# One pass of the index keys' projection folded into unused weight columns, and a turn of the heads' weights moved down the queue

## The chip, the cores and the metric

The kernel runs on one core of a Trainium2 chip. A core has five engines with an instruction queue each, run in order: TensorE (PE, with its weight loads PEld), VectorE (DVE), ScalarE (ACT), GpSimd (POOL) and SyncE (SP, which here only issues DMAs). Times are device microseconds (us) for one execution, from launch to end; lower is better. A profile shows one execution, and its span runs from the first to the last instruction.

## The reference

One transformer block on 512 tokens of width 1024, in float32. Its input projection `u @ w_in` is cut into the parts of three attentions; the second (DSA) is the one that matters here:

```python
aq, ak, av, bq, bkv, biq, bik, biw, cq, ck, cv, g = split_cols(u @ w_in[l])
...
s_idx = jax.nn.relu(jnp.einsum('bqhd,bkd->bqhk', iqb, ik))
score = jnp.einsum('bqhk,bqh->bqk', s_idx, iwb).astype(jnp.float32) * idx_scale
score = jnp.where(causal[None], score, -jnp.inf)
_, sel = lax.top_k(score, topk)
```

`biq` are the index queries (8 heads of 32 columns), `bik` the index keys (32 columns that all heads share), `biw` the weight of each head (8 columns). The scores choose which keys the DSA attention reads, so they are computed to nearly full float32. After the three attentions come their branch products, the output product, a feed-forward part and a last norm.

## The kernel before

Nearly all of the time goes to 128x512 matmuls in float32r. To keep precision, each projection is three passes: the weights and the activations are split into a high and a low half (`wh`, `wl`, `uh`, `ul`), and a pass is `wh*uh`, `wl*uh` or `wh*ul`, summed in one PSUM bank. ACT writes a high half by a copy into float32r, DVE the low half by subtraction.

**The first stage** takes the model dimension in four shares of two 128-row tiles. In a share q the modulation sums (`mod_sums`, DVE and ACT: eight scaled rows summed into `gsum`) are turned into columns by small matmuls (`gps`, L376), DVE makes the factors `ab` from them, ACT makes `uh`, splits the weights (`split_share`) and makes `ut`, DVE makes the low halves and `ul`, and PE runs `b_part` (L456) for three weight tiles of 256 columns: `b0` (banks `p_kv`, `p_iq0`), `b1` (banks `p_iq1`, `p_ik`) and `bq0` (banks `p_bq00`, `p_bq01`). Of the second 128 columns of `b1` only 40 are used: 32 index keys and 8 head weights; the other 88 are computed and read by nobody. While PE runs share q, DVE sums for share q+1.

**Behind the shares** stand, in program order: the copies of the index queries (`put_iq`, with 12 small DMAs each, half on SP and half on POOL, that lay heads side by side in `iqs`), the copies of `p_ik` (`kst` and `kl`, high and low half of the keys, with two DMAs that repeat them on partitions 32 to 95; `iwr`, the head weights), and the two banks of `bq0`. Then PE starts the chunk `bq1`: 48 matmuls (L535, L537, L539). Between them small steps are interleaved, by a queue that `Flow.run` empties:

```python
if self.side and i % 4 == 3:
    self.side.popleft()()
...
flow.side.extend([iw_turn, kv1, kv2, kv3, lambda: None, kv4, kv5])
```

So the first step stands behind the 4th matmul, the next behind the 8th, and so on. `iw_turn` turns the head weights `iwr` on PE (L596, bank tag T, which has one buffer) and copies them to `iw` on DVE. `kv1` turns `kvT` on PE (L612, bank T), `kv2` makes the squares and the root on ACT (L617, L619), `kv3` the reciprocal and `kvt` on DVE (L622, L624), `kv4` turns `kvt` back on PE (L630, bank T), `kv5` writes `kvnT` on DVE. The chunks `c0` to `c2` follow `bq1`, with the index products between their matmuls.

Of the kernel before, what the change touches and what calls it, by code (L numbers as in the profile page):

```python
# [13 lines left out]
F32 = mybir.dt.float32  # L14
F32R = mybir.dt.float32r
AF = mybir.ActivationFunctionType
ALU = mybir.AluOpType
# [109 lines left out]
def block_kernel(ctx: ExitStack, tc: tile.TileContext, x, c, rel_bias, ada_w, ada_b, norm_mix, w_in,  # L127
                 gate_b, diff_lambda, diff_subln, dsa_kv_norm, dsa_w_uv, w_br_a, w_br_b, w_br_c, w_o,
                 norm_mlp, w_ff1, w_ff2, norm_final, onehot, out):
    nc = tc.nc  # L130
# [12 lines left out]
    flow = Flow()  # L143
# [64 lines left out]
    raws, parts = {}, {}  # L208
# [80 lines left out]
    SHARES = ((0, 2), (2, 4), (4, 6), (6, 8))  # L289
# [108 lines left out]
    def split_share(q, names):  # L398
        ks = slice(*SHARES[q])
        for n in names:  # L400
            if n not in parts and n == "b1":
                both = st.tile([128, 2, 8, 256], F32R, name="hl_b1")
                parts[n] = (both[:, 0], both[:, 1])
            elif n not in parts:
                parts[n] = tuple(wp.tile([128, 8, 256], F32R, tag=t, name=f"{t}_{n}") for t in ("hi", "lo"))
            hi, lo = parts[n]
            nc.scalar.activation(hi[:, ks], raws[n][:, ks], AF.Copy)
            nc.vector.tensor_tensor(lo[:, ks], raws[n][:, ks], hi[:, ks].bitcast(F32), op=ALU.subtract)

# [36 lines left out]
    def b_part(n, q, ps=(0, 1, 2)):  # L446

        wh, wl = parts[QS[n]]
        names = (("kv", 0), ("iq0", 1)), (("iq1", 0), ("ik", 1)), (("bq00", 0), ("bq01", 1))
        for p in ps:  # L450
            w, u = ((wh, uh), (wl, uh), (wh, ul))[p]
            products = [(name, j, k) for name, j in names[n] for k in range(*SHARES[q])]
            if n == 0:
                products.sort(key=lambda e: e[2])
            for name, j, k in products:
                nc.tensor.matmul(first[name], w[:, k, j * 128:(j + 1) * 128], u[:, k],  # L456
                                 start=k == 0 and p == 0, stop=k == KT - 1 and p == 2)
                yield
# [10 lines left out]
    mod_columns(0)  # L469
    warm(5)  # L470
    split_share(0, QS[:1])
    make_uh(0)
    split_share(0, QS[1:])
    make_ul(0)
    mod_sums(1, range(4))

    def first_two(q):

        return chain(b_part(0, q, (0, 1)), b_part(1, q, (0, 1)), b_part(0, q, (2,)), b_part(1, q, (2,)))

    for q in range(LAST):
        if q + 2 <= LAST:
            fetch_share(q + 2)
        mod_sums(q + 1, range(4, KT))
        rest = b_part(2, q)
        for _ in chain(first_two(q), islice(rest, 4)):
            pass
        split_share(q + 1, QS[:1])
        if q + 2 <= LAST:
            mod_sums(q + 2, (0, 1))  # L490
        mod_columns(q + 1)
        make_uh(q + 1)
        if q + 2 <= LAST:
            mod_sums(q + 2, (2, 3))
        split_share(q + 1, QS[1:])
        make_ul(q + 1)
        if q + 1 == LAST:
            fetch(3)
            fetch(4)
        for _ in rest:  # L500
            pass
# [13 lines left out]
    def kv_tile(name, dt=F32):  # L515
        return at.tile([128, 512], dt, tag="kv", name=name, bufs=14)

    def p_tile(name, dt=F32):
        return at.tile([128, 512], dt, tag="P", name=name, bufs=5)
# [24 lines left out]
    def proj_chunk(chunk, evacs, when=(2, 5, 7, 12)):  # L544
        use(chunk, when)
        for j in range(2):
            yield from proj(f"p_{chunk}{j}", chunk, j, evacs[j])
# [4 lines left out]
    kst = at.tile([96, 512], F32R, tag="kst", name="kst")  # L552
    kl = p_tile("kl", F32R)
    iwr = p_tile("iwr")
    iw = const.tile([128, 32], F32, name="iw")

    def put_iq(g, p):
        nc.scalar.activation(iqx[:, 2 * g], p, AF.Copy)
        nc.vector.tensor_tensor(iqx[:, 2 * g + 1], p, iqx[:, 2 * g].bitcast(F32), op=ALU.subtract)
        for r in range(4):  # L560
            for b, part in enumerate((0, 1, 0)):
                (nc.gpsimd if r < 2 else nc.sync).dma_start(iqs[32 * b:32 * b + 32, 4 * g + r].bitcast(F32),
                                  iqx[32 * r:32 * r + 32, 2 * g + part, 128:512].bitcast(F32))
# [6 lines left out]
    kvT = kv_tile("kvT")  # L570
    nc.scalar.activation(kvT, first["kv"], AF.Copy)
    p_ik = first["ik"]
    nc.scalar.activation(kst[0:32], p_ik[0:32], AF.Copy)
    nc.vector.tensor_tensor(kl[0:32], p_ik[0:32], kst[0:32].bitcast(F32), op=ALU.subtract)
    nc.scalar.activation(iwr[32:40], p_ik[32:40], AF.Copy, scale=0.0625)
    nc.sync.dma_start(kst[32:64].bitcast(F32), kst[0:32].bitcast(F32))
    nc.sync.dma_start(kst[64:96].bitcast(F32), kl[0:32].bitcast(F32))
    put_iq(1, first["iq1"])
    for _ in b_part(2, LAST):
        pass  # L580

# [2 lines left out]
    def put_bq(i):  # L584
        def evac(p):
            bq[i] = kv_tile(f"bq{i}")
            nc.scalar.activation(bq[i], p, AF.Copy, scale=128 ** -0.5)
        return evac

    put_bq(0)(first["bq00"])  # L590
    put_bq(1)(first["bq01"])

    def iw_turn():
        iwp = bank("T", "iwp")
        for i in range(1, 4):
            nc.tensor.transpose(iwp[:, 8 * i:8 * i + 8], iwr[32:40, i * 128:(i + 1) * 128], ident[32:40, 32:40])  # L596
        nc.vector.tensor_copy(iw[:, 8:32], iwp[:, 8:32])
# [34 lines left out]
    def kv5():  # L632
        nc.vector.tensor_scalar(kvnT, kb["b"], vcol[:, C_KVN:C_KVN + 1], None, op0=ALU.mult)

    flow.side.extend([iw_turn, kv1, kv2, kv3, lambda: None, kv4, kv5])
    flow.run(proj_chunk("bq1", [put_bq(2), put_bq(3)], (14, 18, 26, 32)))


# [952 lines left out]
```

## Time and profile before

| | us |
|---|---|
| median of 3 runs (lowest to highest) | 834.23 (833.16 to 834.74) |
| the profiled execution's own time | 833.88 |
| its span | 832.0 |
| PE busy in the span | 806.9 (97%) |
| DVE, ACT, POOL busy | 570.3, 411.8, 163.6 |

The span is 1.88 us shorter than the execution's own time, which has what lies around the instructions. PE is the busiest engine by far: what delays PE's queue delays the end, unless PE would have waited anyhow. "Busy" counts a matmul from its start to its modelled end, so that back-to-back matmuls overlap; the distance from start to start is what a matmul costs PE.

### The profile page before, as it was taken

How to read it: one execution, taken by the hardware profiler on the slowest of the kernel's cores; microseconds unless marked ns; L12 is line 12 of the kernel's file. 1: busy time of each engine (PE TensorE's matmuls, PEld its weight loads, DVE VectorE, ACT ScalarE, POOL GpSimd, SP SyncE). 2: the span in 40 equal slices, each digit the busy share in tenths (PEclk: the TensorE clock that was granted, in tenths of full speed). 3: DMA queues.
4: the chain of work that ended last, by engine and by line, in shares of the span. 5: the costliest groups of instructions: out<-in, count | busy, mean ns of one | idle time of the engine just before them, and what ended most of it. 6: DMA issues, size and time to landing. Idle time of an engine off the chain costs nothing. (4 is left out here: it accounts for less than half of the span.)

```text
span 832.0 us, 10495 instructions
## 1 busy us (share of the span) xinstructions
PE 806.9 (97%) x3865; PEld 644.7 (77%) x3865; DVE 570.3 (69%) x1004; ACT 411.8 (49%) x712; POOL 163.6 (20%) x118
## 2 busy tenths in 40 slices
PE   5999999999999999999999999999999999999996
PEld 4778877678777776677788789888888888888885
DVE  5865776687878359894454776874678578857554
ACT  7555635452434365455743436545563366334433
POOL 2014332202562225003156460000000000010020
PEclk9999999999999999999999999999999999999998
DMA  9946552134656276421137527114411531173302
GB/s 313 347 134 189 190 196 74 52 102 127 198 183 213 96 267 191 153 89 52 50 103 265 187 68 290 50 51 154 151 50 51 189 129 37 52 252 102 101 1 101
DMA packets 81534, 116.47 MB, mean 140 GB/s; under 512 B 4590, under 2 KB 53274, under 8 KB 81484
## 3 DMA queue, kind: packets, MB, share of 16 engines
q1 hardware_dynamic: 78812, 107.73, 39.5%
q0 software_dynamic: 2672, 8.09, 2.8%
q8 instruction: 30, 0.49, 0.2%
q14 instruction: 20, 0.16, 0.1%
HBM read 110.25 MB, written 8.17 MB: 142 GB/s over the span
## 5 line engine op out<-in xcount | busy, mean ns | idle before, releaser
L1275 PE MATMUL pf<-u2h,hi_f 128*128 128x512 f32 x224 | 87.1, 389 | 0.0
L1277 PE MATMUL pf<-u2l,hi_f 128*128 128x512 f32 x224 | 87.1, 389 | 0.0
L1279 PE MATMUL pf<-u2h,lo_f 128*128 128x512 f32 x224 | 87.1, 389 | 0.0
L956 DVE SCALAR_TENSOR_TENSOR adacc<-adch,cond,adacc 128x512 f32<-128x512 f32 x56 | 59.7, 1065 | 5.2 <-DMA adch<-in_ada_w_dram 4.7
L244 DVE TENSOR_TENSOR lo_f<-raw_f,hi_f 128x1024 fp32r<-128x1024 f32 x38 | 46.6, 1255 | 16.9 <-ACT hi_f L232 16.9
L232 ACT ACTIVATE hi_p<-w 128x1024 fp32r<-128x1024 f32 x36 | 36.3, 1050 | 34.0 <-PE pp L1421 27.0
L244 DVE TENSOR_TENSOR lo_p<-w,hi_p 128x1024 fp32r<-128x1024 f32 x36 | 42.7, 1221 | 9.8 <-ACT hi_p L232 9.8
L232 ACT ACTIVATE hi_f<-raw_f 128x1024 fp32r<-128x1024 f32 x38 | 38.6, 1048 | 21.5 <-PE p2l L1537 7.1
L1279 PEld LDWEIGHTS pf<-u2h,lo_f 128*128 128x128 f32 x224 | 42.0, 188 | 8.8
L1277 PEld LDWEIGHTS pf<-u2l,hi_f 128*128 128x128 f32 x224 | 42.0, 188 | 8.7
L1275 PEld LDWEIGHTS pf<-u2h,hi_f 128*128 128x128 f32 x224 | 42.0, 188 | 8.7
L1445 POOL DMA_DIRECT2D x1f<-x1d x4 | 2.1, 538 | 234.3 <-PE pp L1421 234.3
L1421 PE MATMUL pp<-hi_p,hq 128*128 128x512 f32 x144 | 45.8, 389 | 0.0
L244 POOL TENSOR_TENSOR lo_gb<-raw_gb,hi_gb 128x1024 fp32r<-128x1024 f32 x8 | 20.0, 2524 | 66.0 <-ACT hi_gb L232 66.0
L1421 PEld LDWEIGHTS pp<-hi_p,hq 128*128 128x128 f32 x144 | 27.0, 188 | 5.6
L1421 PE MATMUL pp<-hi_p,ha 128*128 128x512 f32 x96 | 30.5, 389 | 0.0
L1421 PE MATMUL pp<-hi_p,he 128*128 128x512 f32 x96 | 30.5, 389 | 0.0
L735 ACT ACTIVATE Pa<-Pa,nma 128x128 f32<-128x128 f32 (+3 forms) x32 | 17.7, 554 | 24.6 <-DVE nma L731 24.5
L1415 DVE TENSOR_TENSOR acc<-acc,pp 128x512 f32<-128x512 f32 x32 | 21.7, 683 | 10.6 <-PE pp L1421 10.6
L1421 PE MATMUL pp<-lo_p,hq 128*128 128x512 f32 x72 | 28.1, 390 | 0.0
L535 PE MATMUL p_gb<-uh,hi_gb 128*128 128x512 f32 x64 | 27.5, 430 | 0.0
L537 PE MATMUL p_gb<-ul,hi_gb 128*128 128x512 f32 x64 | 26.8, 419 | 0.0
(430 smaller groups left out, 2300.1 us busy)
## 6 DMA issues: line engine op xcount, KB each, us to landing
raw_f<-in_w_ff_dram SPq DMA_DIRECT2D x20, 1024.0 KB, 5.7
adch<-in_ada_w_dram SPq DMA_DIRECT2D x64, 256.0 KB, 3.2
w<-in_w_ff_dram SPq DMA_DIRECT2D x12, 1024.0 KB
ada<-in_ada_w_dram SPq DMA_DIRECT2D x32, 256.0 KB, 6.4
raw_gc<-in_w_in_dram SPq DMA_DIRECT2D x4, 1024.0 KB, 16.9
raw_gb<-in_w_in_dram SPq DMA_DIRECT2D x4, 1024.0 KB, 5.6
raw_a<-in_w_in_dram SPq DMA_DIRECT2D x4, 1024.0 KB
raw_ga<-in_w_in_dram SPq DMA_DIRECT2D x4, 1024.0 KB, 7.6
```

The costliest lines, as they stand in the source:

```text
L232: nc.scalar.activation(parts[n][0][:, sl], raws[n][:, sl], AF.Copy)
L244: eng.tensor_tensor(parts[n][1][:, sl], raws[n][:, sl], parts[n][0][:, sl].bitcast(F32), op=ALU.subtract)
L535: nc.tensor.matmul(dst, wh[:, k, cs], uh[:, k], start=k == 0, stop=False)
L537: nc.tensor.matmul(dst, wh[:, k, cs], ul[:, k], start=False, stop=False)
L735: nc.scalar.activation(p[:, 0:w], p[:, 0:w], AF.Exp, bias=nm, scale=-1.0, accum_out=sm)
L956: nc.vector.scalar_tensor_tensor(acc, ach[n], cond[:, k:k + 1], acc, op0=ALU.mult, op1=ALU.add)
L1275: nc.tensor.matmul(dst, wh[:, i, cs], u2h[:, i], start=i == 0, stop=False)
L1277: nc.tensor.matmul(dst, wh[:, i, cs], u2l[:, i], start=False, stop=False)
L1279: nc.tensor.matmul(dst, wl[:, i, cs], u2h[:, i], start=False, stop=i == KT - 1)
L1415: nc.vector.tensor_tensor(c, c, dst[t], op=op)
L1421: nc.tensor.matmul(dst[t], a[:, part, k, j, ts_], w[:, k], start=not onto and k == 0 and m == 0, stop=k == 3 and m == 2, skip_group_check= ...
L1445: nc.gpsimd.dma_start(x1f[:, t], x1d[t * 128:(t + 1) * 128])
```

## The change

The split of tile `b1` now writes, into the 88 unused columns of the high tile, the low halves of the 40 used ones: columns 192 to 231 of the high tile hold the low half of columns 128 to 167, the rest of columns 168 to 255 is set to zero by POOL once. The first pass over `p_ik` then gives the high product on partitions 0 to 39 and the low product on partitions 64 to 103 of the same bank, and the pass `wl*uh` of `ik` is left out. The two parts have to be added: ACT copies partitions 64 to 103 to `ikl`, a DMA moves them to partitions 0 to 39, and DVE adds (`iks`). The copies that made `kst`, `kl` and `iwr` from `p_ik` now take `iks` (function `put_ik`) and stand behind the two copies of `bq0`. `iw_turn` goes from the front of the side queue to its end. (The third pass, `wh*ul`, now also has a low part; it is a product that was left out before.)

```diff
@@ split_share
+                nc.gpsimd.memset(both[:, 0, :, 168:256].bitcast(F32), 0.0)
...
+            if n == "b1":
+
+                for c0, c1, dst in ((0, 128, lo[:, ks, 0:128]), (128, 168, hi[:, ks, 192:232])):
+                    if c0 == 0:
+                        nc.scalar.activation(hi[:, ks, 0:168], raws[n][:, ks, 0:168], AF.Copy)
+                    nc.vector.tensor_tensor(dst, raws[n][:, ks, c0:c1], hi[:, ks, c0:c1].bitcast(F32), op=ALU.subtract)
+                continue
@@ b_part
-            products = [(name, j, k) for name, j in names[n] for k in range(*SHARES[q])]
+            products = [(name, j, k) for name, j in names[n] for k in range(*SHARES[q]) if (name, p) != ("ik", 1)]
@@ behind the shares
-    nc.scalar.activation(kst[0:32], p_ik[0:32], AF.Copy)
-    nc.vector.tensor_tensor(kl[0:32], p_ik[0:32], kst[0:32].bitcast(F32), op=ALU.subtract)
-    nc.scalar.activation(iwr[32:40], p_ik[32:40], AF.Copy, scale=0.0625)
-    nc.sync.dma_start(kst[32:64].bitcast(F32), kst[0:32].bitcast(F32))
-    nc.sync.dma_start(kst[64:96].bitcast(F32), kl[0:32].bitcast(F32))
+    ikl, iks = p_tile("ikl"), p_tile("iks")
+    nc.scalar.activation(ikl[64:104], p_ik[64:104], AF.Copy)
+    nc.sync.dma_start(ikl[0:40], ikl[64:104])
     put_iq(1, first["iq1"])
+
+    def put_ik():
+
+        nc.vector.tensor_tensor(iks[0:40], p_ik[0:40], ikl[0:40], op=ALU.add)
+        nc.scalar.activation(kst[0:32], iks[0:32], AF.Copy)
+        nc.vector.tensor_tensor(kl[0:32], iks[0:32], kst[0:32].bitcast(F32), op=ALU.subtract)
+        nc.scalar.activation(iwr[32:40], iks[32:40], AF.Copy, scale=0.0625)
+        nc.sync.dma_start(kst[32:64].bitcast(F32), kst[0:32].bitcast(F32))
+        nc.sync.dma_start(kst[64:96].bitcast(F32), kl[0:32].bitcast(F32))
+
...
     put_bq(1)(first["bq01"])
+    put_ik()
...
-    flow.side.extend([iw_turn, kv1, kv2, kv3, lambda: None, kv4, kv5])
+    flow.side.extend([kv1, kv2, kv3, lambda: None, kv4, kv5, iw_turn])
```

The change moves instructions on several queues. On SP, behind the last loads of the first stage, the queue was this (`iqs` are the small DMAs of the index queries, `kst` those of the keys):

```order
L217 DMA raw_c_510<-in_w_in_dram 128x8x256
L562 DMA iqs<-iqx 32x384 x6
L576 DMA kst<-kst 32x512
L577 DMA kst<-kl 32x512
L562 DMA iqs<-iqx 32x384 x6
L217 DMA raw_c_619<-in_w_in_dram 128x8x256
```

and is now this:

```order
L217 DMA raw_c_509<-in_w_in_dram 128x8x256
L570 DMA iqs<-iqx 32x384 x6
L583 DMA ikl<-ikl 40x512
L570 DMA iqs<-iqx 32x384 x6
L592 DMA kst<-kst 32x512
L593 DMA kst<-kl 32x512
L217 DMA raw_c_621<-in_w_in_dram 128x8x256
```

The new transfer of `ikl` stands behind the first six `iqs` transfers, where the first `kst` transfer stood, and the two of `kst` stand behind all twelve.

On ACT, from the copy of `p_kv` to the split of `c0`, before (`kjunk` are the squares of `kv2`):

```order
L571 ACTIVATE kvT<-p_kv 128x512
L573 ACTIVATE kst<-p_ik 32x512
L575 ACTIVATE iwr<-p_ik 8x512
L558 ACTIVATE iqx<-p_iq_245 128x512
L587 ACTIVATE bq_607<-p_bq_247 128x512
L587 ACTIVATE bq_609<-p_bq_248 128x512
L617 ACTIVATE kjunk,kss<-tpk 128x128 x4
L619 ACTIVATE kss<-kss,eps 128x4
```

and now:

```order
L579 ACTIVATE kvT<-p_kv 128x512
L582 ACTIVATE ikl<-p_ik 40x512
L566 ACTIVATE iqx<-p_iq_245 128x512
L603 ACTIVATE bq_603<-p_bq_247 128x512
L603 ACTIVATE bq_605<-p_bq_248 128x512
L589 ACTIVATE kst<-iks 32x512
L591 ACTIVATE iwr<-iks 8x512
L634 ACTIVATE kjunk,kss<-tpk 128x128 x4
L636 ACTIVATE kss<-kss,eps 128x4
```

The two copies out of the keys went from ahead of the second `iqx` copy to the place right ahead of the squares, and they read `iks`. On DVE the sum `iks` and the subtraction `kl` stand, in the same way, right ahead of the reciprocal of `kv3`.

On PE, from the first matmul of `bq1`, before:

```order
L535 MATMUL p_bq_621<-uh,hi_bq_568 128x512
L537 MATMUL p_bq_621<-ul,hi_bq_568 128x512
L539 MATMUL p_bq_621<-uh,lo_bq_569 128x512
L535 MATMUL p_bq_621<-uh,hi_bq_568 128x512
L596 MATMUL iwp<-ident,iwr 128x8 x3
L537 MATMUL p_bq_621<-ul,hi_bq_568 128x512
L539 MATMUL p_bq_621<-uh,lo_bq_569 128x512
L535 MATMUL p_bq_621<-uh,hi_bq_568 128x512
L537 MATMUL p_bq_621<-ul,hi_bq_568 128x512
L612 MATMUL tpk<-ident,kvT 128x128 x4
```

and now:

```order
L543 MATMUL p_bq_623<-uh,hi_bq_565 128x512
L545 MATMUL p_bq_623<-ul,hi_bq_565 128x512
L547 MATMUL p_bq_623<-uh,lo_bq_566 128x512
L543 MATMUL p_bq_623<-uh,hi_bq_565 128x512
L629 MATMUL tpk<-ident,kvT 128x128 x4
L545 MATMUL p_bq_623<-ul,hi_bq_565 128x512
L547 MATMUL p_bq_623<-uh,lo_bq_566 128x512
```

Every step of `kv` stands four matmuls of `bq1` earlier: the first turn behind 4 matmuls instead of 8, the turn back (`kv4`) behind 20 instead of 24, and the head weights' turn behind 28 instead of 4.

## Rows read from the trace of the kernel before

**Rows 1.** The page, part 1: busy us, share of the span, instructions.

```profile
PE 806.9 (97%) x3865; PEld 644.7 (77%) x3865; DVE 570.3 (69%) x1004; ACT 411.8 (49%) x712; POOL 163.6 (20%) x118
```

**Rows 2.** Waits of PE, whole span: us in total, times, longest.

```profile
PE u2p L1247 <- POOL tn L1242: 2.4, 2, 1.6
PE gps L376 <- DVE gsum L368: 2.3, 3, 1.8
```

**Rows 3.** Timeline of PE, first stage: start, us, instruction, idle before and releaser.

```profile
18.02 1.02 PE L376 MATMUL gps<-ones,gsum 128*128 128x1 f32 x8 [0.19 <-DVE gsum L368]
...
29.17 1.02 PE L376 MATMUL gps<-ones,gsum 128*128 128x1 f32 x8 [1.80 <-DVE gsum L368]
...
36.76 0.62 PE L456 MATMUL p_ik<-uh,hl_b 128*128 128x512 f32 x2
37.22 0.39 PE L456 MATMUL p_kv<-ul,hi_b 128*128 128x512 f32 x1
...
49.53 1.02 PE L376 MATMUL gps<-ones,gsum 128*128 128x1 f32 x8 [0.32 <-DVE gsum L368]
```

**Rows 4.** Groups by form, ACT and DVE: busy us, mean ns of one, idle before.

```profile
L407 ACT ACTIVATE hl_b<-raw_b 128x512 fp32r<-128x512 f32 x4 | 2.5, 614 | 0.0
L232 ACT ACTIVATE hi_bq<-raw_bq 128x1024 fp32r<-128x1024 f32 x2 | 2.0, 1050 | 0.0
L408 DVE TENSOR_TENSOR hl_b<-raw_b,hl_b 128x512 fp32r<-128x512 f32 x4 | 2.8, 693 | 5.2 <-ACT hl_b L407 5.2
L244 DVE TENSOR_TENSOR lo_bq<-raw_bq,hi_bq 128x1024 fp32r<-128x1024 f32 x2 | 2.4, 1223 | 0.3 <-ACT hi_bq L232 0.3
```

**Rows 5.** Timeline of PE, chunk bq1 up to the first matmul of c0.

```profile
60.51 0.39 PE L535 MATMUL p_bq<-uh,hi_bq 128*128 128x512 f32 x1
...
62.28 0.35 PE L596 MATMUL iwp<-ident,iwr 8*128 8x8 f32 x3 [0.71 <-ACT iwr L575]
...
67.87 0.60 PE L630 MATMUL tpk<-ident,kvt 128*128 128x128 f32 x4
...
68.55 0.39 PE L537 MATMUL p_bq<-ul,hi_bq 128*128 128x512 f32 x1
...
73.77 0.39 PE L535 MATMUL p_c<-uh,hi_c 128*128 128x512 f32 x1
```

**Rows 6.** Timeline of SP behind the shares: issue of the small DMAs.

```profile
57.71 3.78 SPq L562 DMA_DIRECT2D iqs<-iqx  x6
61.67 0.51 SPq L576 DMA_DIRECT2D kst<-kst  x1
```

**Rows 7.** Transfers of tile iqs (24 of 48 KB): issue to landing.

```profile
DMA to landing us min/median/max: 1.8/2.0/2.1
```

**Rows 8.** Timelines of ACT and of DVE behind the shares.

```profile
61.64 0.59 ACT L575 ACTIVATE iwr<-p_ik 8x512 f32<-8x512 f32 x1 [1.12 <-DVE kl L574]
...
64.42 0.28 ACT L617 ACTIVATE kjunk<-tpk 128x128 f32<-128x128 f32 x1 [0.58 <-PE tpk L612]
...
60.94 0.67 DVE L574 TENSOR_TENSOR kl<-p_ik,kst 32x512 fp32r<-32x512 f32 x1
...
66.56 1.13 DVE L624 TENSOR_SCALAR kvt<-tpk,kss 128x128 f32<-128x128 f32 x4
```

**Rows 9.** Windows of PE: stretch, length, busy (instructions), granted clock (1.00 is full), DMA share, GB/s.

```profile
27.00:31.00 4.00, 2.20 (x14) 1.00 1.09 348
31.00:35.00 4.00, 4.00 (x12) 0.57 1.09 347
479.00:483.00 4.00, 4.00 (x22) 1.00 0.02 4
824.30:826.60 2.30, 0.00 (x0) 1.00 0.55 204
826.80:832.00 5.20, 0.00 (x0) 0.50 0.53 199
```

**Rows 10.** A memset of POOL, in groups by form.

```profile
L600 POOL MEMSET cmask<- 128x512 f32 x1 | 0.5, 546 | 0.0
```

## Prediction

> **What bounds the kernel now.** I read the page first: PE is busy for 97% of the span [rows 1], so a change of 2 us has to be looked for in PE's queue. Next the waits of PE over the whole span: they are few, and two are long, the turn of `u2` far behind the change and the `gps` matmuls, which wait for DVE's sums in the first stage [rows 2]. The reader is to see there that the stage in which the matmuls are removed is one of the few in which PE waits. Then the timelines of PE: first the four shares, then the chunk `bq1`, in which PE stood 0.71 us for the head weights [rows 3, 5]; and those of SP, ACT and DVE behind the shares, to see what the new transfer waits for and who waits for it [rows 6, 8].
>
> **The matmuls removed.** Eight go, two in each share. The pair of the second share starts at 36.76 and the next matmul at 37.22 [rows 3]: 0.23 us each at full clock, 0.46 a share, 1.84 in all. How much of it arrives is another matter.
>
> Share 1. PE waits 1.80 us for `gsum` at 29.17 [rows 3]. Two matmuls less make that wait longer; what counts is when DVE is done. DVE's sums stand behind the low half of `b1`, for which DVE waits on ACT's copy in every share [rows 4]. That copy shrinks from 512 to 336 elements: from 614 ns at 512 and 1050 ns at 1024 [rows 4] an element costs 0.85 ns, so 0.15 us are saved. On DVE 512 elements become 256 and 80; from 693 and 1223 ns [rows 4], 1.04 ns an element, they cost 0.43 and 0.25, the same as the 0.69 before. So the wait ends 0.15 earlier: gain 0.15.
>
> Share 2. PE does not wait for `gsum` at its end: the three waits of [rows 2] are those at 18.02, 29.17 and 49.53 [rows 3]. The 0.46 arrives. Sum 0.6.
>
> Share 3. PE waited 0.32 us at 49.53 [rows 3], so DVE ended last, and again only ACT's 0.15 counts. Sum 0.75, and PE's wait there grows to about 0.6.
>
> Share 4. Nothing of DVE stands between: 0.46 arrives. Sum 1.2. So `bq1`, which began at 60.51 [rows 5], begins at 59.3. Bounds: 0.9 (second share DVE-bound too) and 1.84 (no wait at all).
>
> POOL's memset (704 elements; 546 ns for 512 [rows 10], so some 0.75 us by proportion) lies in POOL's idle time before the first use of the tile. I take it at nothing; if DVE's sums stood still for all of it, the first share would begin 0.75 later.
>
> **The turn moved.** At `iw_turn` PE stood 0.71 us and worked 0.35 [rows 5]. Behind the 28th matmul the weights are there, and only the 0.35 is paid. That saves 0.7, if nothing else waits.
>
> **What is added.** `iks` needs both parts on the same partitions, so the path is ACT copy, SP issue, transfer, DVE sum. The transfer takes the slot in SP's queue in which `kst` was issued, at 61.67, because the six `iqs` issues ahead of it take 3.78 us [rows 6]. They wait for `iqx`, which moves with PE: 61.67 - 1.2 = 60.47. ACT's copy of `ikl` is ready before that. Of its landing no row shows anything; the nearest is that of `iqs`, 1.8 to 2.1 us from the issue for 48 KB [rows 7]. It carries 80 KB, so I take the upper end, 2.1: 62.57. [...]
>
> Then DVE adds: 0.67 like `kl`, which reads the same bank [rows 8], to 63.24. ACT now has the copies `kst` and `iwr` right ahead of the squares of `kv2`, and its queue is in order: two operations of the length of `iwr` (0.59 each [rows 8], less some 0.09 by which neighbours overlap) end the wait of the squares at 63.28 + 1.0 = 64.28. Before they began at 64.42, and `kvt` ended at 66.56 + 1.13 = 67.69 [rows 8], 3.27 later. So now `kvt` ends at 67.55, and the turn back (`kv4`), which stood 0.18 behind it, starts at 67.7. That is hardly earlier than the 67.87 of before [rows 5].
>
> But PE comes to it much earlier, since it now stands behind 20 matmuls, not 24, and no longer behind the head weights. A group of four transposes costs 68.55 - 67.87 - 0.23 = 0.45 [rows 5]. PE arrives at 59.3 + 20 x 0.227 + 0.45 = 64.3 and stands till 67.7: by the trace's way of counting (to a matmul's modelled end, 0.16 more) **an idle time of about 3.2 us**. Queued behind the waiting transposes are the 28 other matmuls of `bq1` and everything after. ACT's squares wait for `kst`, `kst` for `iks`, `iks` for the transfer: that is the new chain.
>
> From there to the first matmul of `c0`: 0.45 + 28 x 0.227 + 0.35 = 7.16, so 74.86, against 73.77 [rows 5]. **The removed work and the removed wait are paid back with 1.1 us on top.** Break-even needs the turn back at 66.6, 1.1 us earlier than I have it.
>
> Later needs have cover: `kst` is repeated by 68, and the index products that read it start behind `c0`'s first matmuls; the head weights are read later still.
>
> **The clock.** After the 1.80 us wait and the tiny `gps` matmuls behind it, PE's granted clock fell from full to half for part of 31 to 35, mean 0.57 [rows 9]: 4 x 0.43 = 1.7 us lost. After the 1.6 us wait [rows 2] in front of 478 it did not fall (1.00 from 479 to 483), and behind PE's last work it was still full from 824.3 to 826.6 and at 0.50 from 826.8 on [rows 9]. A pure wait of 3.2 us is twice the one that passed without a fall, and longer than the idle 2.5 us after which it fell at the end; most likely it brings the half level again. What it takes back is between nothing and 1.7; part of a slow stretch may fall into the idle time itself, so I take 1.5. [...]
>
> **Sum.** 833.88 + 1.1 + 1.5 = 836.5. The profiled execution lies 0.35 under the median of the three runs, 834.23; a measurement of this kernel tells 0.2%, 1.7 us, from no change, so slower begins at 835.9 and faster at 832.6.
>
> **Rivals.**
> - *The wait comes, the clock holds.* [...] Time 833.88 + 1.1 = 835.0, no change by the measure. Chance 0.25.
> - *The transfer is early enough* (the other side). If SP issues `ikl` ahead of the `iqs` transfers' end, or it lands in far less than 2 us, so that `kv4` finds `kvt` by 64.3, PE keeps 1.2 + 0.7 + 0.4 (the head weights' wait had also delayed the matmuls around it): about 831.6. It decides at a turn back before 66.6. Against it: six issues of 0.6 us stand ahead on the same queue [rows 6]. Chance 0.07.
> - *The clock falls twice.* The wait in front of the fourth share grows from 0.32 to 0.6; with the `gps` matmuls behind it that is nearer to the stretch in which it fell at 31. Another 1.6: 838.1. Against it: the wait of 1.80 that led to a fall was three times as long. Chance 0.08.
> - *The removed matmuls bring nothing in any share* (all DVE-bound): `bq1` 0.9 later than I have it, but the chain of `ikl` moves with it; 837.4. Included in the forecast's upper half.
>
> **How the numbers follow.** The forecast (wait and one fall of the clock) has 0.60, with a range of its own of 835.7 to 837.5 from the bounds of the shares and of the clock's price. The first rival has 0.25, the second 0.07, the third 0.08. Of the forecast nine tenths lie above 835.9, all of the third, and a tenth of the first: 0.65 slower. The second is faster, 0.07; the remaining 0.28 is no change. The range takes in most of the first rival and ends short of the third's far side: 834.2 to 838.0.
>
> **What would show it.** In the profile after: the wait of PE for `iwr` gone; a wait of some 3 us at the turn of `kvt`, put down to DVE; ACT idle ahead of `kst`, DVE idle ahead of `iks` until a DMA; waits for `gsum` of about 2.1 and 0.6; granted clock near 0.5 in some 3 us behind the turn. The prediction is wrong if the landing of `ikl` comes before 61, if PE's wait there is under 2 us, or if the half clock does not come back.

## The result and the profile after

The changed kernel takes 840.0 us in the median (839.19 to 840.91, 6 runs) against 833.88 (832.22 to 836.64) for the kernel before on the same chip: ratio 1.0070, 95% interval 1.0059 to 1.0082. Slower, as forecast, but 3.5 us more than forecast and outside the range. The profiled execution took 839.53 us; its span is 837.7.

The busy times of the page; PE's hardly differs from [rows 1]:

```profile
span 837.7 us, 10493 instructions
PE 807.2 (96%) x3857; PEld 644.9 (77%) x3857; DVE 571.2 (68%) x1009; ACT 412.2 (49%) x713; POOL 164.2 (20%) x119
```

The waits of PE, which answer to [rows 2]:

```profile
PE tpk L647 <- DVE kvt L641: 5.3, 1, 5.3
PE gps L376 <- DVE gsum L368: 3.5, 3, 2.1
```

One new wait of 5.3 us at the turn back, and more waiting for `gsum`. The wait for `iwr` is gone. The same view of the kernel before has two waits of PE that are longer than those of [rows 2], and that the prediction passed over:

```profile
PE xtp L336 <- DVE xt L330: 5.3, 2, 4.6
PE cps L411 <- DMA crow<-in_c_dram: 2.3, 1, 2.3
```

Both lie ahead of the shares, and the changed kernel has them with 4.5 and 2.3 us, so the difference between the kernels does not come from them.

The timeline of PE, for [rows 3, 5]:

```profile
30.16 1.02 PE L376 MATMUL gps<-ones,gsum 128*128 128x1 f32 x8 [2.11 <-DVE gsum L368]
39.70 1.02 PE L376 MATMUL gps<-ones,gsum 128*128 128x1 f32 x8 [0.67 <-DVE gsum L368]
49.23 1.02 PE L376 MATMUL gps<-ones,gsum 128*128 128x1 f32 x8 [0.67 <-DVE gsum L368]
59.74 0.39 PE L543 MATMUL p_bq<-uh,hi_bq 128*128 128x512 f32 x1
...
64.54 0.39 PE L545 MATMUL p_bq<-ul,hi_bq 128*128 128x512 f32 x1
70.18 1.11 PE L647 MATMUL tpk<-ident,kvt 128*128 128x128 f32 x4 [5.25 <-DVE kvt L641]
...
79.43 0.39 PE L543 MATMUL p_c<-uh,hi_c 128*128 128x512 f32 x1
```

The chunk `bq1` begins 0.8 us earlier than before, `c0` 5.66 us later (79.43 against 73.77). The spans differ by 5.7, so all of the loss lies between the two. The windows of PE (length, PE busy and instructions, granted clock, DMA share, GB/s):

```profile
63.00:67.00 4.00, 1.93 (x9) 1.00 0.49 131
67.00:71.00 4.00, 0.82 (x5) 0.55 0.52 116
71.00:75.00 4.00, 4.00 (x14) 0.59 0.66 226
75.00:79.00 4.00, 4.00 (x19) 1.00 0.42 98
```

In windows of 1 us the granted clock is 0.50 in each from 68 to 74. Read with the means, full clock ends at about 67.4, in the middle of the wait, and comes back at about 74.3: for some 4.1 us, from the turn back at 70.18 on, PE works at half clock (from 71.52 its matmuls start 0.43 us apart, before the wait 0.23). The chain that PE waits for, in the timelines of SP, DVE and ACT, against [rows 6, 8]:

```profile
56.94 4.71 SPq L570 DMA_DIRECT2D iqs<-iqx  x6
61.89 0.83 SPq L583 DMA_DIRECT2D ikl<-ikl  x1
...
64.71 0.68 DVE L588 TENSOR_TENSOR iks<-p_ik,ikl 40x512 f32<-40x512 f32 x1 [3.45 <-DMA iqs<-iqx]
...
65.43 0.63 ACT L589 ACTIVATE kst<-iks 32x512 fp32r<-32x512 f32 x1 [3.91 <-DVE iks L588]
66.08 0.63 ACT L591 ACTIVATE iwr<-iks 8x512 f32<-8x512 f32 x1
66.73 0.28 ACT L634 ACTIVATE kjunk<-tpk 128x128 f32<-128x128 f32 x1
```

The trace names `iqs` as the releaser of `iks`; no operand of that sum is `iqs`, so the transfer is `ikl`'s (in the version with the turn back later the trace names `ikl`, after a wait of 3.43 us). ACT stands 3.91 us, and the squares `kjunk` come 2.3 us later than before. SP's `iqs` issues in two rows (number, shortest, median and longest issue in ns; issue to landing in us), where [rows 7] had at most 2.1:

```profile
L570 SPq DMA_DIRECT2D iqs<-iqx x12: 524/590/1494, 56.9 to 66.0; - x12
DMA to landing us min/median/max: 1.9/2.6/3.4
```

### The profile page after: what moved, and what is told of

It is laid out like the page before. It is cut to its first block, busy times and chain, and to the rows that moved or that the text cites. A ratio compares the mean times of both kernels' runs of the same rounds, so it can differ in the third digit from the quotient of the medians.

```text
span 837.7 us, 10493 instructions
## 1 busy us (share of the span) xinstructions
PE 807.2 (96%) x3857; PEld 644.9 (77%) x3857; DVE 571.2 (68%) x1009; ACT 412.2 (49%) x713; POOL 164.2 (20%) x119
```

## The experiments

Theory: the turn back waits for a chain through one small transfer, which stands ahead of `kv2` in ACT's queue, and the clock falls behind that wait. Rivals: the loss is in the shares or in the turn's new place, or the half clock comes in any case. Each ratio is to the kernel before on the same chip, which has a median between 833.88 and 834.30 on each of the chips used. A measure that holds for all kernels: from the start of `c0` to the end of the span every profile has 758.1 to 758.6 us, so the first 72 to 80 us decide. Divided at the first matmul of the shares and at the first of `bq1`, and with the first stage's clock (in brackets the lowest mean granted clock of the windows of 4 us from 20 to 60), the profiles give (us, in the order of the sections below):

| | shares | `bq1` | clock in the shares |
|---|---|---|---|
| before | 40.04 | 13.26 | fell (0.65) |
| changed | 38.12 | 19.69 | full (1.00) |
| copies behind kv3 | 40.47 | 12.70 | fell (0.52) |
| turn moved, alone | 39.05 | 13.91 | full (1.00) |
| pass left out, alone | 38.01 | 13.24 | fell at the first matmuls (0.54) |
| no transfer | 40.47 | 13.99 | fell (0.55) |
| transfer on ACT's queue | 38.81 | 17.46 | fell (0.67) |
| PE kept busy | 38.85 | 17.22 | fell (0.71) |
| turn back later | 38.16 | 13.70 | full (0.99) |
| shares filled | 38.17 | 12.67 | full (1.00) |
| shares filled, before | 39.04 | 13.29 | full (1.00) |

So with a full clock the shares take 39.05 us with the pass and 38.15 in the versions with the changed split and without the pass: 0.9 is what the two give there.

### The copies behind kv3

```diff
-    put_ik()
...
-    flow.side.extend([kv1, kv2, kv3, lambda: None, kv4, kv5, iw_turn])
+    flow.side.extend([kv1, kv2, kv3, put_ik, kv4, kv5, iw_turn])
```

> The changed kernel with the copies out of the keys (the sum iks, kst, kl, iwr and the two transfers) moved from ahead of the squares to the place behind kv3, in the empty step of the side queue. Theory (the keys' copies, which wait for the transfer, hold up the squares in ACT's in-order queue and so the turn back): the 5.3 us wait of PE at the turn of kvt shrinks to about 0.5, the half clock there goes, and what is left is the gain of the shares: about 832, with a possible wait of up to 1 us at the head weights' turn. Rival (the turn back is too early behind 20 matmuls whatever stands ahead of the squares): PE still waits 2 us or more at kvt and the time stays above 835.

833.07 us (ratio to before 0.9994, 0.9982 to 1.0005). The transfer, the sum and the copies are the same instructions; they only stand behind the squares on ACT and behind `kvt` on DVE. From the timelines:

```profile
62.53 0.30 ACT L633 ACTIVATE kjunk<-tpk 128x128 f32<-128x128 f32 x1
...
65.92 0.66 PE L646 MATMUL tpk<-ident,kvt 128*128 128x128 f32 x4
66.49 0.63 ACT L589 ACTIVATE kst<-iks 32x512 fp32r<-32x512 f32 x1 [1.10 <-DVE iks L588]
```

The turn back finds `kvt` ready, and the median is 6.9 us under that of the changed kernel. So what cost the time was the place of the copies in two in-order queues. The loss is gone, but a gain over the kernel before is not shown: the interval takes in 1. The profile also holds a fall of the clock, in the second share:

```profile
27.00:31.00 4.00, 2.04 (x9) 0.75 1.09 351
31.00:35.00 4.00, 4.00 (x10) 0.50 1.09 346
```

### The turn moved, alone

```diff
-    flow.side.extend([iw_turn, kv1, kv2, kv3, lambda: None, kv4, kv5])
+    flow.side.extend([kv1, kv2, kv3, lambda: None, kv4, kv5, iw_turn])
```

> The kernel before with only the side queue's order of the changed one (the head weights' turn last, every kv step four matmuls earlier). Theory (moving the kv steps up is itself a loss, since kvt is not ready behind 20 matmuls): PE's 0.7 us wait for iwr goes and a wait of about 1.5 us at the turn of kvt comes; 834.5 to 835. Rival (the turn's move is a gain and the loss is all of the transfer's): no wait of over 0.5 us at kvt, about 833.

835.17 (1.0017, 1.0006 to 1.0029), all else as before:

```profile
61.02 0.59 ACT L575 ACTIVATE iwr<-p_ik 8x512 f32<-8x512 f32 x1 [1.12 <-DVE kl L574]
...
63.09 0.30 ACT L617 ACTIVATE kjunk<-tpk 128x128 f32<-128x128 f32 x1
...
66.42 0.66 PE L630 MATMUL tpk<-ident,kvt 128*128 128x128 f32 x4 [1.34 <-DVE kvt L624]
```

The head weights' wait of 0.7 went, and 1.34 came at the turn back, four matmuls earlier in PE's queue. `bq1` to `c0` grew from 13.26 to 13.91 us. With the copies out of the keys ahead of the squares, as before, this edit is a loss by itself: the squares begin 3.2 us behind the first matmul of `bq1` (63.09 - 59.89). In the first experiment, with the same turn and the copies behind it, they begin 1.65 us behind it (62.53 - 60.88), and PE does not wait.

### The pass left out, alone

```diff
-            products = [(name, j, k) for name, j in names[n] for k in range(*SHARES[q])]
+            products = [(name, j, k) for name, j in names[n] for k in range(*SHARES[q]) if (name, p) != ("ik", 1)]
```

> The kernel before without the pass of the index keys' and head weights' low halves (it leaves that product out; nothing stands in for it, no other edit). Theory (in the first and third share DVE's sums end last, so half of the removed matmuls' 1.84 us turns into longer waits): 0.9 us off, 833.0. Rival (all of it arrives): 832.0; other rival (the longer waits bring the half clock): no gain.

The kernel before with only this line; it leaves the product `wl*uh` of the keys out. 833.89 (0.9999, 0.9989 to 1.0008): the expected gain did not show. Two of the waits in the shares:

```profile
40.30 1.02 PE L376 MATMUL gps<-ones,gsum 128*128 128x1 f32 x8 [0.78 <-DVE gsum L368]
49.97 1.02 PE L376 MATMUL gps<-ones,gsum 128*128 128x1 f32 x8 [0.79 <-DVE gsum L368]
```

In the run with the turn alone, whose clock stayed full in the shares (1.00 from 16 to 60), these two stand so with all matmuls in place:

```profile
39.21 1.02 PE L376 MATMUL gps<-ones,gsum 128*128 128x1 f32 x8 [0.34 <-DVE gsum L368]
48.89 1.02 PE L376 MATMUL gps<-ones,gsum 128*128 128x1 f32 x8 [0.36 <-DVE gsum L368]
```

The distance is 9.67 us here and 9.68 there, and the waits are 0.44 and 0.43 longer here: the removed matmuls became waits. Only the last share, which no sum follows, could give its 0.46. In this profile the clock fell already around the first matmuls (granted 0.60 in 16 to 20, 0.54 in 20 to 24), so that PE came late to the first wait (1.40 us); the 38.01 of the table cannot be compared with the other versions.

### No transfer

```diff
-    nc.scalar.activation(ikl[64:104], p_ik[64:104], AF.Copy)
-    nc.sync.dma_start(ikl[0:40], ikl[64:104])
+    nc.scalar.activation(ikl[0:40], p_ik[0:40], AF.Copy, scale=0.0)
```

> The changed kernel without the transfer: ACT fills ikl[0:40] with zeros from the same bank in place of the copy and the DMA, so the low half's product is left out of the keys and head weights; all other instructions stand where they stood. Theory (the slot in SP's queue and the landing make most of the lateness): the sum iks starts at about 61.3 instead of 64.7, kvt ends at about 66.7, PE still waits some 1.5 to 2 us and the clock may hold; 834 to 835.5. Rival (the copies' place alone makes the wait): the wait stays above 4 us and the time above 838.

`ikl` is zero, so the low product is left out of the sum. 834.5 (1.0006, 0.9994 to 1.0018):

```profile
61.75 0.67 DVE L587 TENSOR_TENSOR iks<-p_ik,ikl 40x512 f32<-40x512 f32 x1
...
67.22 0.66 PE L646 MATMUL tpk<-ident,kvt 128*128 128x128 f32 x4 [1.43 <-DVE kvt L640]
```

PE's wait falls from 5.25 to 1.43 and the clock stays full behind it (1.00 from 64 to 76), with the copies still ahead of `kv2`. So the transfer and its slot make 3.8 us of the wait. The rest is near the 1.34 of the moved turn alone and has the same cause: the squares begin 3.2 us behind `bq1` here too (63.77), since the copies still stand ahead of them.

### The transfer on ACT's queue

```diff
-    nc.sync.dma_start(ikl[0:40], ikl[64:104])
+    nc.scalar.dma_start(ikl[0:40], ikl[64:104])
```

> The changed kernel, with the transfer of ikl issued on ACT's queue, right behind ACT's copy of ikl, and not behind the six iqs issues on SP's. Theory (SP's queue is a large part of the chain): ikl is issued at about 60 and not at 61.9, iks starts at about 62.5 and not at 64.7, and the turn back (kv4) waits about 3 us and not 5.3. If the clock falls behind it as before, about 837.5; if the shorter wait lets it stand, about 835.5. Rival (the landing of the transfer is what is slow, whichever queue it is on, because it shares the DMA engines with the loads and the iqs transfers): iks starts after 64 and the time stays at about 840.

837.46 (1.0036, 1.0023 to 1.0049), as the theory had it. The timelines of ACT's queue, DVE and PE:

```profile
60.29 1.31 ACTq L583 DMA_DIRECT2D ikl<-ikl  x1
...
63.12 0.68 DVE L588 TENSOR_TENSOR iks<-p_ik,ikl 40x512 f32<-40x512 f32 x1 [0.15 <-DMA ikl<-ikl]
...
68.59 0.98 PE L647 MATMUL tpk<-ident,kvt 128*128 128x128 f32 x4 [3.33 <-DVE kvt L641]
```

Issued 1.6 us earlier, the transfer takes 2.83 us to the sum, as on SP (2.82). So SP's queue was worth 2 us of the wait (3.33, not 5.25), and the landing was long on either queue. The clock fell again (0.72 in 67 to 71), behind a wait of 3.3 us.

### PE kept busy

```diff
     def kv4():
+        held = bank("O", "held")
+        for _ in range(22):
+            nc.tensor.matmul(held[:, 0:128], ident, ident, start=True, stop=True)
         kb["b"] = bank("T", "tpk2")
```

> The changed kernel, with 22 calls of a 128x128 matmul of the identity, whose result nobody reads, right ahead of the turn back (kv4): about 5.1 us of work of no use in the time in which PE waited. The chain to kvt is the same. Theory (the idle time makes the clock fall, and the fall costs 2.1 us beyond it): granted clock 1.00 in 67 to 79, c0 begins some 2 us earlier against bq1, time about 838. Rival (the half clock there is one that this stretch gets in any case): clock at 0.5 to 0.6 behind the turn back again, time 840 or more, since the matmuls of no use then last longer than the wait.

838.41 (1.0046, 1.0030 to 1.0062), 1.6 us under the changed kernel with 44 instructions more. Timeline and windows of PE:

```profile
64.18 5.07 PE L647 MATMUL held<-ident 128*128 128x128 f32 x44
69.09 0.60 PE L650 MATMUL tpk<-ident,kvt 128*128 128x128 f32 x4
```

```profile
67.00:71.00 4.00, 4.00 (x32) 1.00 0.70 192
71.00:75.00 4.00, 4.00 (x20) 1.00 0.53 152
```

The wait is filled and the half clock does not come. `bq1` to `c0` is 17.22 us, not 19.69; of the 2.47, 0.54 come from an earlier turn back (9.90 us behind the start of `bq1`, not 10.44). From the turn back to `c0` it is 7.32 us, not 9.25: 1.93 is the price of the half clock. In these two profiles the fall thus goes with PE's standing still, and it is a term of its own; this rests on one profile of each kernel.

### The turn back later

```diff
-    flow.side.extend([kv1, kv2, kv3, lambda: None, kv4, kv5, iw_turn])
+    flow.side.extend([kv1, kv2, kv3] + [lambda: None] * 6 + [kv4, kv5, iw_turn])
```

> The changed kernel, with the turn back (kv4), kv5 and iw_turn placed behind 40, 44 and 48 matmuls of bq1 and not behind 20, 24 and 28; the chain of ikl, iks, kst, kvt is not touched. Theory (only PE's place in its own order was wrong: the chain may be as long as it is if PE has other work): PE arrives at the turn back at about 69.3, waits under 1 us, the clock stays full, and c0 begins about 13.2 us behind bq1 and not 19.7: 833 to 834. Rival (c0 or the index products then wait for kvnT or iw, or for kst): a new wait behind c0's first matmuls and 835.5 or more.

833.66 (0.9998, 0.9984 to 1.0013), with the chain as long as in the changed kernel (six `iqs` issues in 4.74 us, ACT's wait for `iks` 3.89):

```profile
71.18 0.66 PE L647 MATMUL tpk<-ident,kvt 128*128 128x128 f32 x4 [0.70 <-DVE kvt L641]
...
74.20 0.32 PE L613 MATMUL iwp<-ident,iwr 8*128 8x8 f32 x3 [0.52 <-DVE kvnT L650]
```

Twenty matmuls between hide most of the chain: 0.70 us of wait is left, and a new one of 0.52 has come at the head weights' turn, so that `c0` begins 13.70 us behind `bq1`, not the 13.2 expected. From `c0` on PE does not wait for what now comes later.

### The shares filled

```diff
+        warm((8, 2, 2)[q])
         mod_columns(q + 1)
```

> The version with put_ik behind kv3, with 8, 2 and 2 calls of a 128x128 matmul of the identity, whose result nobody reads, in front of the gps matmuls of the second, third and fourth share: about 1.9, 0.5 and 0.5 us of work of no use, inside waits of 2.1, 0.7 and 0.7 us. Theory (in the executions in which the clock falls behind the first of these waits, it costs 1 to 2 us, and the wait is what makes it fall): granted clock 1.00 from 27 to 39 in the profile, no time lost in the shares, median 1 us under 833.1, at about 832.2, and runs closer together. Rival (the fall is not made by the wait, or costs nothing in the median): 833.1 or more with the spread as before.

Added to the first experiment's kernel. 831.7 (831.37 to 832.35; ratio 0.9966, 0.9953 to 0.9979): this is below both kernels. PE's waits at `gps` and the windows:

```profile
29.23 1.02 PE L376 MATMUL gps<-ones,gsum 128*128 128x1 f32 x8 [0.28 <-DVE gsum L368]
38.76 1.02 PE L376 MATMUL gps<-ones,gsum 128*128 128x1 f32 x8 [0.19 <-DVE gsum L368]
...
71.52 0.39 PE L544 MATMUL p_c<-uh,hi_c 128*128 128x512 f32 x1
```

```profile
27.00:31.00 4.00, 3.72 (x29) 1.00 1.09 350
31.00:35.00 4.00, 4.00 (x19) 1.00 1.10 349
```

The six runs have a mean granted clock of 0.998 each and lie within 1 us, where the same kernel without the fill had 0.989 to 0.998 and a spread of 3.7 us in twelve runs on another chip.

### The shares filled, before

```diff
+        warm((7, 1, 1)[q])
         mod_columns(q + 1)
```

> The kernel before, with 7, 1 and 1 calls of a 128x128 matmul of the identity, whose result nobody reads, in front of the gps matmuls of the second, third and fourth share: nothing else is changed. It says how much of the gain of the version with put_ik behind kv3 and filled shares (831.7) comes from the change and how much from the clock alone. Theory (nearly all of it is the clock of the shares, and the change itself, with put_ik behind kv3, gives only the 0.46 of the last share and part of the 0.7 wait for the head weights): granted clock 1.00 from 27 to 39, 832.2 to 832.8. Rival (the change itself gives the gain, and the matmuls of no use give none): 833.9 as before.

834.21 against 834.30 on its chip (1.0004, 0.9992 to 1.0016): the theory falls here. The clock is full in the shares of this profile (1.00 from 16 to 60), as it had it, and the median does not move.

```profile
30.23 1.02 PE L376 MATMUL gps<-ones,gsum 128*128 128x1 f32 x8 [0.23 <-DVE gsum L368]
...
73.87 0.39 PE L536 MATMUL p_c<-uh,hi_c 128*128 128x512 f32 x1
```

From the first matmul of the shares to `c0` this kernel takes 73.87 - 21.54 = 52.33 us, the filled new one 71.52 - 20.68 = 50.84. So 1.49 us of the difference between the two are the change's own: 39.04 - 38.17 = 0.87 in the shares, 13.29 - 12.67 = 0.62 in `bq1`. Why the fill alone gives nothing is not settled. Of the twelve runs with the fill eight have a mean granted clock of 0.997 or more, of the 17 of before on that chip four; but the median span is 832.1 us against 832.4, and six of the twelve take 2.3 to 3.0 us outside their spans, where those of before take at most 1.93. In its one profile with a fall the kernel before lost 1.0 us; with the pass removed four profiles lost 0.7, 0.7, 2.3 and 2.3. Whether the removed pass, with its longer wait (2.11 us, not 1.79), makes the falls more frequent is not shown: on one chip 15 of 35 runs of before had a mean granted clock of 0.997 or more, and 3 of 24 of the first and the third experiment's kernels, both without the pass; but the turn alone, which has the pass, had 3 of 12 there.

## Why the forecast was right in sign and too small

**Confirmed.** The wait for `iwr` gone; PE waiting at the turn back for `kvt`; DVE's `iks` waiting for a transfer and ACT's `kst` for `iks`; `gps` waits of 2.1 and 0.67 where "about 2.1 and 0.6" was written; the half clock behind the turn back; the removed and regained time paid back with more on top.

**The first step that failed: the size of the wait.** "An idle time of about 3.2 us" was 5.25. Measured from the start of `bq1`, the turn back came at 10.44 instead of 67.7 - 59.3 = 8.4. The terms:

| | predicted | measured |
|---|---|---|
| `bq1` to the issue of `ikl` | 1.17 | 2.15 |
| issue to the sum `iks` | 2.10 | 2.82 |
| `iks` to the squares | 1.71 | 2.02 |
| squares to the turn back | 3.42 | 3.45 |

SP needed 4.71 us for the six `iqs` issues, not 3.78: one took 1.49. The landing was priced by the slowest of the neighbours in one profile of before, 2.1; in this profile these landed in up to 3.4 us on SP's queue. And the copies, 0.63 each, did not overlap. The mechanism held: the version with the transfer on ACT's queue takes the first term away and keeps the second, and the copies behind `kv3` take the whole wait away. From issue to sum the transfer took 2.58 to 2.82 us in three versions on SP's queue and 2.83 on ACT's.

**The second: the clock's price.** "I take 1.5": from the turn back to `c0` the trace has 9.25 us, at full clock it would be the predicted 7.16, so 2.1 (with PE kept busy 7.32 was measured, so 1.93). The prediction took the slow stretch to be as long as the one at 31 and part of it to fall into the idle time; it lasted some 6.9 us, and 4.1 of these fell on work. Three profiles bear out that it falls with waits of this length (with those of 5.25 and 3.33 it fell, to means of 0.55 and 0.72 from 67 to 71; with the wait filled it stayed at 1.00); with the waits of 1.34 and 1.43 in `bq1` it did not fall (1.00 from 64 to 76). The bound "between nothing and 1.7" came from one fall in the shares; those cost from 0.7 to 2.3 by the table.

**The third, small: "Share 2. ... The 0.46 arrives."** It did not. In the profile of before PE was late there because its clock had fallen; at full clock DVE is last in shares 1 to 3, and the removed matmuls went into waits. Arrived were 0.9 us, the lower bound: 0.15 by ACT's shorter copy in each of three shares (from one `gps` to the next 9.54 and 9.53 us, where all matmuls or the pass alone left out gave 9.68 and 9.67) and 0.46 in the last. POOL's memset, "I take it at nothing", held: of the kernels that have it, four begin the shares at 20.13 to 20.68, the kernel before at 20.47.

**The sum.** From `bq1` to `c0` the prediction had 74.86 + 1.5 - 59.3 = 17.06, the trace 19.69: 2.6 us, of which 2.0 is the wait and 0.6 the clock. With the 0.3 that the shares gave less than forecast (0.9, not 1.2) that is 2.9 of the 3.5 by which the forecast was too low. Against before's 13.26 that is 6.43; less the 0.9 gained in the shares 5.5, and the medians differ by 6.1. Where the other 0.6 lies is not shown; it is within what the start of the first stage differs by from one execution to the next (the first matmul of the shares came at 20.47 before and at 21.62 in the changed kernel).

**Rivals.** "The transfer is early enough" fell: `iks` began at 64.71. "The clock holds" fell. "The clock falls twice" did not happen in the profile: its wait in front of the fourth share grew to 0.67, and the clock stayed full behind it:

```profile
48.00:52.00 4.00, 3.33 (x19) 1.00 0.27 53
```

That "the removed matmuls bring nothing in any share" fell too, by the 0.9.

## What to carry over

When a value has to change partitions by a small transfer, keep its readers behind the work that others wait for in every in-order queue: the same instructions cost 6.9 us ahead of the squares and nothing behind `kvt`. Do not price such a transfer by one profile: the slowest landing and the slowest issue of its neighbours were 2.1 and 0.61 us in the profile of before, and 3.4 and 1.49 in the next. The waits of PE of 3.3 and 5.3 us cost their length and a slow stretch behind it (mean clock 0.72 from 67 to 71 and 0.59 from 71 to 75), those of 1.3 and 1.4 their length alone (1.00), and behind those of 2.1 in the shares the clock fell in some profiles (means of 0.60 to 0.90 from 28 to 32 in four) and not in others (1.00 in two). Work removed from PE in a stage where another engine ends last came back here as a wait (of 0.46 us a share, 0.44 and 0.43 in the second and the third, with DVE last).

## What was not expected of the hardware

- One `iqs` issue on SP took 1.49 us where the median is 0.59, and the landings behind it up to 3.4 us; the kernel before has 0.61 and 2.1 at most. A slow issue (1.03 to 1.54 us) is in seven of the eight profiles without the pass, among them that of the kernel before with only the pass left out, so it is not the new transfer's doing; the three profiles with the pass have none over 0.62. What makes it stays open.
- Falls of the clock in the first stage differ from execution to execution of the same code. Of the profiles whose code is the changed kernel's up to there, four have one behind the first `gps` wait, at 28 to 36, one already at 16 to 22, and one none. Filling 2 us of waiting with useless matmuls went with a spread of 1.0 us (six runs) where the kernel without had 3.7 (twelve, on another chip); in the kernel before the like fill left 4.7 us.
